# Depthwise convolution of a decoder trunk: shifted copies read from a DRAM copy of U, three buffers deep

## The chip, the cores and the metric

The kernel runs on one core of a Trainium2 chip. The metric is the device time of one execution in microseconds. Three runs of the kernel before took 2775.14, 2775.54 and 2778.75 us, median 2775.54 us.

## The reference

One inference step of a four-layer trunk for a prompt of 512 positions and for 8 decode streams of 4 positions each: 544 columns of 1024 channels. Layers 0 and 3 have a Conformer convolution as mixer, layer 1 latent attention, layer 2 retention; each layer then has a SwiGLU block. The change lies in the convolution, which is this:

```python
a = h @ w_pw1 + b_pw1
u = a[..., :D_MODEL] * jax.nn.sigmoid(a[..., D_MODEL:])
buf = jnp.concatenate([buf_prev.astype(u.dtype), u], axis=1)
c = lax.conv_general_dilated(buf, w_dw[:, None, :], (1,), 'VALID', ..., feature_group_count=D_MODEL) + b_dw
c = jax.nn.silu(_layernorm(c, ln_g, ln_b))
return c @ w_pw2 + b_pw2, buf[:, -(CONV_WIDTH - 1):]
```

Each of the 1024 channels has 31 taps of its own (CONV_WIDTH is 31); everything is in float32.

## The kernel before

Channels lie on the partitions, in eight tiles m = 0 to 7 of 128; columns lie along the free dimension. A column range is cut into two halves, h = 0 and h = 1, of 272 columns. A full-precision product is made of three passes over operands that ScalarE and VectorE have split into a high and a low part (`wsplit`, lines 196 and 197).

`conv` runs in four stages.

1. The first pointwise product (line 216, tiles `pg` and `pa`) makes U, one tile m after another: 835 columns per channel, which hold the padded prompt and the eight decode windows with their 30 past rows (lines 826 and 828 write it). Meanwhile VectorE computes the taps of tiles 0 and 1 by multiply-add (line 846).
2. The taps of the other tiles go through TensorE. `windows(m, h)` makes S, a tile of 128 partitions by 4 groups of 32 channels: for each group g one DMA on SyncE's queue reads 32 partitions of U four times, each time one column further, so that partition 4c+s holds channel c shifted by s (line 860). A matmul with a 128x32 matrix of taps (W, line 868) then sums four taps at a time, and eight matmuls for each of four groups make 31 taps (line 896). For h = 1 S has 560 columns, since it holds the decode windows too (four copies of 280 KB), for h = 0 it has 300 (four of 150 KB), and for tiles 0 and 1 only the decode windows are copied (four of 144 KB, line 882 alone). The pool gives S of h = 0 and S of h = 1 two buffers each: a copy into one of them starts when the matmuls that read it last are done.
3. Each result leaves its PSUM bank by VectorE (line 909), is squared on ScalarE (line 915) and goes into two running sums (lines 913 and 916). `moments(h)` turns these into mean and variance (ones-matmuls of lines 924 and 925, then lines 926 to 930 and `rsqrt`, lines 261 to 265); `normed` normalises a tile, applies silu and splits it (lines 937 to 943). Four PSUM banks go round among all of these.
4. The second pointwise product: four tiles with h = 0 alone first (lines 1548 to 1550, tile `pw2h`), moments and normalisation of h = 1 beside them, then the rest (tile `pw`).

TensorE's order around the convolutions is: decode window of tile 0, (2,0), (3,0), decode window of tile 1, (4,0), (5,0), (6,0), (2,1), (3,1), moments of h = 0, (4,1), (5,1), (6,1), (7,1), `pw2h` of tile 0, moments of h = 1; a pair is (m, h). Half (7,0) is made by VectorE, whose 31 multiply-adds are strewn between its other work (line 846). A framework sets each engine's order and its semaphores from the order of the code; each engine then runs its list strictly in order. SyncE's list also has the weight loads (line 188, two `raw` buffers).

Of the kernel before, what the change touches and what calls it, by code (L numbers as in the profile page):

```python
# [15 lines left out]
F = mybir.dt.float32  # L16
# [7 lines left out]
P = 128  # L24
D = 1024
KD = D // P
# [17 lines left out]
UW = SW + 3  # L44
# [92 lines left out]
class Trunk:  # L137
# [306 lines left out]
    def ffn(self, l, last, order):  # L444
# [14 lines left out]
        with ExitStack() as es:  # L459
# [97 lines left out]
            def four(w, f, put):  # L557
# [12 lines left out]
                def whole(out, op, x, y):  # L570
                    def sums():
                        a[out] = self.xsp.tile([P, 1024], F, tag="xs", name="S").rearrange("p (k c) -> p k c", k=4)
                        op(a[out], a[x], a[y])
# [183 lines left out]
    def conv(self, l, j):  # L757
        tc, nc, A, O = self.tc, self.nc, self.A, self.O
# [1 line left out]
        w2 = A["conv_w_pw2"][j].rearrange("(k p) c -> p k c", p=P)  # L760
        halves = (slice(0, HF), slice(HF, T))
        xs, R = self.enter(lambda k: self.col("norm_mix", l * KD + k))
        with tc.tile_pool(name=f"cv{j}", bufs=1) as cp:

            U = cp.tile([P, KD, UW], F, name="U")
            us = U[:, :, U0:SW].rearrange("p m (b q) -> p m b q", b=NB)
# [41 lines left out]
            for mp in range(0, KD, 2):  # L808
                rg = self.wload(w1[:, :, D + mp * P:D + (mp + 2) * P], KD, 256)
                ra = self.wload(w1[:, :, mp * P:(mp + 2) * P], KD, 256)  # L810
                for q in range(2):
                    m = mp + q
# [40 lines left out]
            def windows(m, h):  # L853

                c0, c1 = ((0, HF + 28), (HF, SW))[h]
                S = cp.tile([P, 4, c1 - c0], F, tag="S" + "AB"[h], name="S", bufs=2)
                a0 = U0 if h and m in CONV_DVE else c0
                for g in range(4):
                    src = U[g * 32:(g + 1) * 32, m, a0:c1]
                    nc.sync.dma_start(S[:, g, a0 - c0:], bass.AP(src.tensor, src.offset, [list(src.ap[0]), [1, 4], [1, c1 - a0]]))  # L860
                return S

            Ws = {}

            def diagonals(m):
                if m not in Ws:
                    W = self.wsp.tile([P, 1024], FR, tag="ws", name="W")[:, :].bitcast(F).rearrange("p (a b) -> p a b", a=32)
                    nc.vector.tensor_mul(W, diag.unsqueeze(1).to_broadcast([P, 32, 32]),
                                         tapst[:, m].rearrange("p g j -> p (g j)").unsqueeze(2).to_broadcast([P, 32, 32]))
                    Ws[m] = W  # L870
                return Ws[m]
# [5 lines left out]

            def sample(m, W, S, out):
                for i in range(8):
                    for g in range(4):  # L880
                        ss = S[:, g, U0 - HF:].rearrange("p (b q) -> p b q", q=SU)[:, :, 4 * i:4 * i + NT]
                        nc.tensor.matmul(out[g * 32:(g + 1) * 32, :], lhsT=W[:, g * 8 + i, :], rhs=ss, start=(i == 0), stop=(i == 7))

            def convolved(m, h):
# [6 lines left out]
                if on_pe:  # L891
                    W, S = diagonals(m), windows(m, h)
                    b = self.bank("cv")
                    for i in range(8):
                        for g in range(4):
                            nc.tensor.matmul(b[g * 32:(g + 1) * 32, :n], lhsT=W[:, g * 8 + i, :],  # L896
                                             rhs=S[:, g, 4 * i:4 * i + n], start=(i == 0), stop=(i == 7))
                    if h:
                        sample(m, W, S, b[:, n:HF])
# [46 lines left out]
            for i, m in enumerate(CO):  # L946
                if m < 7:
                    by_taps(7, 0, HF, range(at, at + SPR[i]))
                    at += SPR[i]
                if m in CONV_DVE:  # L950
                    b = self.bank("cvs")
                    sample(m, diagonals(m), windows(m, 1), b[:, :NS])
                    nc.scalar.activation(cc[m][:, TP:], b[:, :NS], AF.Identity, bias=bias(m))
                convolved(m, 0)
                if m == 0:
                    convolved(m, 1)
# [54 lines left out]
            for h in range(2):  # L1011
                b, s = self.bank("cpo"), self.bank("cso")
                for q in range(4):
                    m = h * 4 + q
# [886 lines left out]
```

## Time and profile before

| | before |
|---|---|
| median of three runs | 2775.54 us |
| profiled execution, its own time | 2779.04 us |
| its span in the trace | 2777.3 us |
| PE (TensorE) busy | 2725.3 us, 98% |
| DVE (VectorE) busy | 1912.0 us, 69% |
| ACT (ScalarE) busy | 1171.0 us, 42% |
| POOL (GpSimd) busy | 129.3 us, 5% |
| DMA of S from U, of the chain that ended last | 1% |
| SyncE's issue of line 860, of that chain | 1% |

A share of the span is a mean over stages with different limits. TensorE is busy for 98% of the whole, mostly with SwiGLU. The two convolution stages take a small part of the span, from about 128 to 206 us and from about 2264 to 2344 us, and what bounds them must be read there.

### The profile page before, as it was taken

What the parts mean: (1) busy time and instruction counts of PE and PEld (TensorE: products, weight loads), DVE (VectorE), ACT (ScalarE), POOL (GpSimd) and SP (SyncE); (2) the same over time, 40 slices, a digit from 0 to 9 for tenths busy, and PEclk for the clock granted to TensorE, in tenths of its full rate; (3) what the DMA queues carried; (4) which work ended last, traced back from release to release, by engine and by line L of the source; (5) the groups of instructions that cost most, each with busy time, mean ns of one, the idle gap of its engine ahead of it and who ended that gap; (6) DMA issues with size and microseconds to landing.
All of it is one profiled execution on the core that took longest, in us unless ns stands there. A gap on an engine that the chain in (4) does not pass through costs nothing.

```text
span 2777.3 us, 52103 instructions
## 1 busy us (share of the span) xinstructions
PE 2725.3 (98%) x22390; PEld 2550.4 (92%) x22390; DVE 1912.0 (69%) x2782; ACT 1171.0 (42%) x1713; POOL 129.3 (5%) x217
## 2 busy tenths in 40 slices
PE   8989999999999999999999999999999999999998
PEld 7969999998779999998888897999999977999998
DVE  6976667676775666677656565766667796756676
ACT  4145343454554343444434343534434315524445
POOL 1000000003420000000100000000000000000000
PEclk9999999999999999999999999999999999999999
DMA  5354332224333233223534334423232444423222
GB/s 158 108 136 138 100 98 92 92 76 140 95 113 107 91 94 105 92 74 104 171 116 158 131 131 136 151 79 107 92 100 68 116 122 129 138 77 107 93 84 86
DMA packets 220892, 305.64 MB, mean 110 GB/s; under 512 B 14911, under 2 KB 153484, under 8 KB 220630
## 3 DMA queue, kind: packets, MB, share of 16 engines
q1 hardware_dynamic: 209036, 266.84, 31.3%
q0 software_dynamic: 11328, 33.59, 3.6%
q8 instruction: 176, 2.88, 0.4%
q10 hardware_dynamic: 298, 1.88, 0.2%
q14 instruction: 54, 0.44, 0.0%
HBM read 256.51 MB, written 24.01 MB: 101 GB/s over the span
## 4 chain that ended last, share of the span: by engine, by line
PE 93%; DMA 3%; DVE 2%; SPq 1%; ACT 1%; issue 0%; ACTq 0%; DVEq 0%
PE p L216 28%; PE x L553 24%; PE pg L216 7%; PE pqk L216 3%; PE pa L216 3%; PE pwo L216 3%; PE pw L216 2%; PE po L216 2%; PE cv L896 2%; DMA S<-U 1%; PE pd L216 1%; PE pv L1548 1%; PE pv L1549 1%; PE pv L1550 1%; PE ob L1783 1%; SPq L860 1%
## 5 line engine op out<-in xcount | busy, mean ns | idle before, releaser
L484 ACT CAST wh<-raw 128x1024 fp32r<-128x1024 f32 (+1 forms) x236 | 241.3, 1022 | 411.9 <-PE p L216 267.7
L472 DVE TENSOR_TENSOR wl<-raw,wh 128x1024 fp32r<-128x1024 f32 (+1 forms) x236 | 279.5, 1184 | 76.1 <-ACT wh L484 75.6
L196 ACT CAST wh<-raw 128x1024 fp32r<-128x1024 f32 (+2 forms) x170 | 160.7, 949 | 378.7 <-PE pg L216 83.5
L216 PE MATMUL p<-gh,wl 128*128 128x272 f32 x1344 | 297.8, 288 | 0.0
L216 PE MATMUL p<-gh,wh 128*128 128x272 f32 x1344 | 297.1, 288 | 0.0
L553 PE MATMUL x<-Bh,wh 128*128 128x272 f32 x1792 | 296.9, 287 | 0.0
L553 PE MATMUL x<-Bh,wl 128*128 128x272 f32 x1792 | 296.8, 287 | 0.0
L216 PE MATMUL p<-gl,wh 128*128 128x272 f32 x1344 | 296.8, 288 | 0.0
L553 PE MATMUL x<-Bl,wh 128*128 128x272 f32 x1792 | 296.8, 287 | 0.0
L216 PE MATMUL p<-xs,wh 128*128 128x272 f32 x1536 | 256.9, 289 | 4.1 <-DVE t L295 4.1
L484 ACT CAST wh<-S 128x1024 fp32r<-128x1024 f32 x128 | 134.9, 1054 | 279.5 <-PE p L216 147.1
L553 PEld LDWEIGHTS x<-Bh,wh 128*128 128x128 f32 x1792 | 251.7, 188 | 0.0
L553 PEld LDWEIGHTS x<-Bh,wl 128*128 128x128 f32 x1792 | 251.5, 188 | 0.0
L553 PEld LDWEIGHTS x<-Bl,wh 128*128 128x128 f32 x1792 | 251.5, 188 | 0.0
L197 DVE TENSOR_TENSOR wl<-raw,wh 128x1024 fp32r<-128x1024 f32 (+2 forms) x170 | 185.4, 1094 | 73.8 <-ACT wh L196 54.7
L299 DVE TENSOR_TENSOR x<-p,x 128x544 f32<-128x544 f32 x152 | 110.0, 724 | 179.9 <-PE p L216 179.5
L216 PEld LDWEIGHTS p<-xs,wh 128*128 128x128 f32 x1536 | 217.5, 188 | 5.1 <-issue 2.8
L216 PEld LDWEIGHTS p<-gh,wh 128*128 128x128 f32 x1344 | 218.7, 188 | 0.0
L216 PEld LDWEIGHTS p<-gl,wh 128*128 128x128 f32 x1344 | 218.6, 188 | 0.0
L216 PEld LDWEIGHTS p<-gh,wl 128*128 128x128 f32 x1344 | 217.7, 189 | 0.0
L472 DVE TENSOR_TENSOR wl<-S,wh 128x1024 fp32r<-128x1024 f32 x128 | 156.6, 1223 | 70.9 <-ACT wh L484 70.9
L216 PE MATMUL pg<-xs,wh 128*128 128x272 f32 x1024 | 179.5, 293 | 5.2 <-ACT wh L196 5.2
(539 smaller groups left out, 5394.9 us busy)
## 6 DMA issues: line engine op xcount, KB each, us to landing
raw<-in_ffn_w SPq DMA_DIRECT2D x86, 1024.0 KB, 5.1
raw<-in_ffn_w SPq DMA_DIRECT2D x72, 512.0 KB, 3.9
raw<-in_conv_w_pw SPq DMA_DIRECT2D x28, 1024.0 KB, 5.6
state<-in_state_ret SPq DMA_DIRECT2D x32, 512.0 KB, 4.9
out_ret_state_sample<-state POOLq DMA_DIRECT2D x32, 512.0 KB, 3.6
S<-U SPq DMA_DIRECT2D x48, 280.0 KB, 5.4
raw<-in_ffn_w SPq DMA_DIRECT2D x16, 768.0 KB, 4.5
raw<-in_ret_w_v SPq DMA_DIRECT2D x8, 1024.0 KB, 5.0
```

What stands on the lines that cost most here:

```text
L196: self.nc.scalar.copy(hv, raw)
L197: self.nc.vector.tensor_sub(lv, raw, hv.bitcast(F))
L216: nc.tensor.matmul(ps[:M, h, :HF], lhsT=w[:, k, :], rhs=x[:, h * HF:(h + 1) * HF], start=(j == 0 and i == 0), stop=(j == n - 1 and i == 2))
L299: self.nc.vector.tensor_add(x, ps[:, :, :HF], x)
L472: nc.vector.tensor_sub(out, a, flat(h))
L484: nc.scalar.copy(job.w[0], src())
L553: nc.tensor.matmul(out[:, t, :HF], lhsT=a[:, k, m], rhs=b[:, k, :], start=(first and i == 0 and k == 0), stop=(i == 2 and k == 3), skip_gr ...
L860: nc.sync.dma_start(S[:, g, a0 - c0:], bass.AP(src.tensor, src.offset, [list(src.ap[0]), [1, 4], [1, c1 - a0]]))
L896: nc.tensor.matmul(b[g * 32:(g + 1) * 32, :n], lhsT=W[:, g * 8 + i, :], rhs=S[:, g, 4 * i:4 * i + n], start=(i == 0), stop=(i == 7))
L1548: nc.tensor.matmul(out, lhsT=ah, rhs=bh, start=start, stop=False)
L1549: nc.tensor.matmul(out, lhsT=ah, rhs=bl, start=False, stop=False)
L1550: nc.tensor.matmul(out, lhsT=al, rhs=bh, start=False, stop=stop)
```

## The change

`conv` gets a pool in DRAM with eight buffers. The first time that `windows` is called for a tile m, GpSimd's queue copies the whole tile of U (128 partitions by 835 columns, 428 KB) into one of them; the four copies of S, still on SyncE's queue, read the same elements from there. S has three buffers for each half instead of two. Lines after 863 move by three.

```diff
-        with tc.tile_pool(name=f"cv{j}", bufs=1) as cp:
+        with tc.tile_pool(name=f"cv{j}", bufs=1) as cp, tc.tile_pool(name=f"ud{j}", bufs=KD, space=bass.MemoryType.DRAM) as dp:
...
-                S = cp.tile([P, 4, c1 - c0], F, tag="S" + "AB"[h], name="S", bufs=2)
+                S = cp.tile([P, 4, c1 - c0], F, tag="S" + "AB"[h], name="S", bufs=3)
                 a0 = U0 if h and m in CONV_DVE else c0
+                if m not in Ud:
+                    Ud[m] = dp.tile([P, UW], F, tag="ud", name="ud")
+                    nc.gpsimd.dma_start(Ud[m], U[:, m, :])
                 for g in range(4):
-                    src = U[g * 32:(g + 1) * 32, m, a0:c1]
+                    src = Ud[m][g * 32:(g + 1) * 32, a0:c1]
                     nc.sync.dma_start(S[:, g, a0 - c0:], bass.AP(src.tensor, src.offset, [list(src.ap[0]), [1, 4], [1, c1 - a0]]))
                 return S
 
-            Ws = {}
+            Ws, Ud = {}, {}
```

SyncE's list in layer 0, before, from the copies for (2,0) to the weights of the second product; 300 columns are h = 0, 560 are h = 1:

```order
L860 DMA S<-U 128x1x300 x4
L188 DMA raw<-in_conv_w_pw 128x8x256
L860 DMA S<-U 128x1x300 x4
L188 DMA raw<-in_conv_w_pw 128x8x256 x3
L860 DMA S<-U 128x1x560 x4
L860 DMA S<-U 128x1x300 x8
L860 DMA S<-U 128x1x560 x4
L860 DMA S<-U 128x1x300 x4
L860 DMA S<-U 128x1x560 x16
L188 DMA raw<-in_conv_w_pw 128x8x256 x4
```

The same stretch of SyncE's list after the change; 288 columns are the decode windows of tile 1:

```order
L863 DMA S<-ud 128x1x300 x4
L188 DMA raw<-in_conv_w_pw 128x8x256
L863 DMA S<-ud 128x1x300 x4
L188 DMA raw<-in_conv_w_pw 128x8x256
L863 DMA S<-ud 128x1x288 x4
L863 DMA S<-ud 128x1x560 x4
L863 DMA S<-ud 128x1x300 x4
L188 DMA raw<-in_conv_w_pw 128x8x256 x2
L863 DMA S<-ud 128x1x560 x4
L863 DMA S<-ud 128x1x300 x8
L863 DMA S<-ud 128x1x560 x16
```

The copies for (2,1) and (4,0), which stood behind the first two loads of the second product's weights, now stand ahead of them; behind them follow (3,1), then (5,0) and (6,0), then (4,1) to (7,1). The decode windows of tile 1 stood earlier in the list and now stand behind (3,0). In layer 3 the list is the same.

GpSimd's list at the same place, before:

```order
L769 MEMSET U 128x8x3
L771 MEMSET U 128x8x2 x8
L779 MEMSET taps 128x8
L1020 DMA out_conv_state_prompt<-pr 30x1024
L1022 DMA out_conv_state_sample<-sr 4x1024 x8
```

and after:

```order
L771 MEMSET U 128x8x2 x8
L779 MEMSET taps 128x8
L860 DMA ud<-U 128x835 x8
L1023 DMA out_conv_state_prompt<-pr 30x1024
L1025 DMA out_conv_state_sample<-sr 4x1024 x8
```

The eight copies of U, in the order of tiles 0, 2, 3, 1, 4, 5, 6, 7, stand where GpSimd had nothing between the clearing of U's margins and the output of the convolution's state. VectorE's and ScalarE's lists keep their order; TensorE's keeps it but for one matmul of `pw2h`, which stood three matmuls into (7,1) and now stands behind it.

## Rows read from the trace of the kernel before

**Rows 1.** The page, part 1: busy time, share of the span, instructions.

```profile
PE 2725.3 (98%) x22390; PEld 2550.4 (92%) x22390; DVE 1912.0 (69%) x2782; ACT 1171.0 (42%) x1713; POOL 129.3 (5%) x217
```

**Rows 2.** Waits of SyncE's queue: who waited for whom, total us, times, longest.

```profile
SPq L860 <- PE cvs L882: 33.4, 4, 16.2
SPq L860 <- PE cv L882: 31.6, 5, 13.2
```

**Rows 3.** Timeline of VectorE, layer 0: start, us, instruction, idle before and its releaser.

```profile
151.12 2.10 DVE L846 SCALAR_TENSOR_TENSOR cc<-U,taps,cc 128x272 f32<-128x272 f32 x4
157.78 0.50 DVE L909 SCALAR_TENSOR_TENSOR cc<-cv,vec,K 128x272 f32<-128x272 f32 x1 [4.55 <-PE cv L896]
...
165.40 0.50 DVE L909 SCALAR_TENSOR_TENSOR cc<-cv,vec,K 128x272 f32<-128x272 f32 x1 [1.76 <-PE cv L882]
...
173.72 0.50 DVE L909 SCALAR_TENSOR_TENSOR cc<-cv,vec,K 128x272 f32<-128x272 f32 x1 [1.90 <-PE cv L882]
...
179.96 0.50 DVE L909 SCALAR_TENSOR_TENSOR cc<-cv,vec,K 128x272 f32<-128x272 f32 x1 [1.88 <-PE cv L882]
...
186.12 0.50 DVE L909 SCALAR_TENSOR_TENSOR cc<-cv,vec,K 128x272 f32<-128x272 f32 x1 [1.01 <-PE cv L882]
...
192.70 0.50 DVE L909 SCALAR_TENSOR_TENSOR cc<-cv,vec,K 128x272 f32<-128x272 f32 x1 [3.45 <-PE cv L882]
```

**Rows 4.** The same timeline in layer 3.

```profile
2281.59 0.50 DVE L909 SCALAR_TENSOR_TENSOR cc<-cv,vec,K 128x272 f32<-128x272 f32 x1 [1.60 <-PE cv L896]
...
2294.55 0.50 DVE L909 SCALAR_TENSOR_TENSOR cc<-cv,vec,K 128x272 f32<-128x272 f32 x1 [4.41 <-PE cv L896]
...
2302.17 0.50 DVE L909 SCALAR_TENSOR_TENSOR cc<-cv,vec,K 128x272 f32<-128x272 f32 x1 [1.76 <-PE cv L882]
...
2312.17 0.50 DVE L909 SCALAR_TENSOR_TENSOR cc<-cv,vec,K 128x272 f32<-128x272 f32 x1 [3.58 <-PE cv L882]
...
2316.77 0.50 DVE L909 SCALAR_TENSOR_TENSOR cc<-cv,vec,K 128x272 f32<-128x272 f32 x1 [0.24 <-PE cv L882]
...
2325.70 0.50 DVE L909 SCALAR_TENSOR_TENSOR cc<-cv,vec,K 128x272 f32<-128x272 f32 x1 [3.77 <-PE cv L882]
...
2330.87 0.50 DVE L909 SCALAR_TENSOR_TENSOR cc<-cv,vec,K 128x272 f32<-128x272 f32 x1 [2.04 <-PE cv L882]
```

**Rows 5.** Timeline of TensorE, layer 0; one convolution window is 64 records of line 896.

```profile
130.47 7.54 PE L896 MATMUL cv<-S,W 128*32 128x272 f32 x128
137.82 0.77 PE L882 MATMUL cvs<-S,W 128*32 128x32 f32 x64
...
161.36 3.45 PE L896 MATMUL cv<-S,W 128*32 128x240 f32 x64
...
165.29 0.72 PE L924 MATMUL s<-S,ones 128*128 128x272 f32 x2
...
195.59 0.62 PE L924 MATMUL s<-S,ones 128*128 128x272 f32 x2
```

**Rows 6.** DMA from 160 to 184 us, copies of S alone: rate, queue's engine share.

```profile
DMA packets 1941, 3.93 MB, mean 164 GB/s; under 512 B 208, under 2 KB 208, under 8 KB 1938
...
q1 hardware_dynamic: 1938, 3.88, 77.4%
```

**Rows 7.** The same from 64 to 70 us, a weight load from DRAM.

```profile
DMA packets 1979, 2.03 MB, mean 338 GB/s; under 512 B 69, under 2 KB 1977, under 8 KB 1977
```

**Rows 8.** Instructions on tile S: time from a copy's issue to its landing.

```profile
DMA to landing us min/median/max: 2.8/4.9/7.7
```

**Rows 9.** The page, part 6: GpSimd's stores of retention state, KB each, us to landing.

```profile
out_ret_state_sample<-state POOLq DMA_DIRECT2D x32, 512.0 KB, 3.6
```

**Rows 10.** Timeline of SyncE's queue in the first product of layer 0.

```profile
83.68 2.52 SPq L860 DMA_DIRECT2D S<-U  x4
88.92 24.33 SPq L188 DMA_DIRECT2D raw<-in_conv_w_pw  x3
```

**Rows 11.** The chain that ended last, there.

```profile
110.65 6.03 PE pa L216 x48
```

## The prediction

> **What bounds the kernel now.** The page comes first, and it misleads: TensorE is busy 98% of the span [rows 1], so an edit to copies seems worth nothing. The waits of SyncE's queue say where to look: the copies of S (line 860) waited 33.4 + 31.6 = 65.0 us for matmuls of the convolution, nine times [rows 2]. With two buffers, a copy starts only when the window two places earlier has been consumed, and TensorE then waits for that copy: a ring.
>
> The next view is VectorE's timeline in the convolution stages, since every window leaves PSUM through VectorE's line 909 and every later step hangs on the sums. Up to 153.22 us (151.12 + 2.10) VectorE works without a row of idle time from the stage's start. From there it sits idle six times in layer 0, each time ended by TensorE's last matmul of a window: 4.55 + 1.76 + 1.90 + 1.88 + 1.01 + 3.45 = 14.55 us [rows 3]. In layer 3 it is seven times: 1.60 + 4.41 + 1.76 + 3.58 + 0.24 + 3.77 + 2.04 = 17.40 us [rows 4]. So VectorE waits for TensorE, and TensorE waits for copies.
>
> TensorE's timeline shows what windows cost when S is there. Two windows with h = 0 take from 130.47 to 137.82 us, 3.68 each; one with h = 1, its decode part included, from 161.36 to 165.29, 3.93 us; a decode window alone 0.77 [rows 5].
>
> **The change, step by step.** The third buffer lets a copy start one window earlier. I follow layer 0 with the orders as they are built, on the axis of the old trace.
>
> TensorE, if S is there: the decode part of tile 1 ends at 137.82 + 0.77 = 138.6; (4,0), (5,0), (6,0) end at 138.6 + 3 x 3.68 = 149.6; (2,1) and (3,1) at 157.5. The moments of h = 0 then wait for the sum over all tiles, which VectorE finishes 4.4 us after 153.22 (an estimate: line 909 of (6,0), the last multiply-adds and two sums, ten instructions of about 0.4), so about 157.7; with some 1.2 us for four ones-matmuls, (4,1) starts at 158.9, and (4,1) to (7,1) end at 162.8, 166.7, 170.7 and 174.6.
>
> VectorE, if its idle times go: the next line 909 comes as early as the work before it allows. The work between two waits is the distance of their rows less the wait: 165.40 - 1.76 - 157.78 = 5.86, then 6.42, 4.36, 5.15 and 3.13 us [rows 3]. So line 909 runs at 153.22 for (6,0), 159.1 for (3,1), 165.5 for (4,1), 169.9 for (5,1), 175.0 for (6,1) and 178.1 for (7,1). TensorE is ahead each time, by 3.6, 1.6, 2.7, 3.2, 4.3 and 3.5 us. So all 14.55 us of idle time go, VectorE is the bound of the stage, and what is late next is VectorE's own work.
>
> The copies, if they land in time. From the end of the window that frees a buffer to the start of the one that needs it there are: (5,0), freed by (2,0) at 134.1, needed at 142.3, 8.2 us; (6,0) 8.1; (4,1) 20; (5,1), freed by (2,1) at 153.5, needed at 162.8, 9.3; (6,1) 9.2; (7,1), freed by (4,1) at 162.8, needed at 170.7, 7.9. No row shows a copy of S from DRAM, so I bound it. From below, the present copies: 164 GB/s at 77.4% of the engines' time, or 212 GB/s with the engines always busy [rows 6]; four copies of 280 KB, 1.147 MB, take 5.4 us, and with the shortest landing of a single copy, 2.8 us [rows 8], 8.2 us. From above, a weight load from DRAM: 338 GB/s [rows 7], so 3.4 + 2.8 = 6.2 us. I take 338, since the source is the same memory, and keep 212. At 338 every slack holds. At 212 the three last copies queue on the engines: (6,1) lands at about 167.1 and (7,1) at 172.5, 0.4 and 1.8 us after TensorE wants them, but VectorE asks for those windows at 175.0 and 178.1, 3.93 us after the latest start that does no harm (171.1 and 174.2). So either pace gives the same time: the third buffer is what pays, the source is not.
>
> [...]
>
> The added copies of U: eight of 428 KB per layer, on GpSimd's queue. The nearest row is a store of 512 KB from that queue, 3.6 us from issue to landing [rows 9]; from below it cannot gain anything, since a copy of S now waits for it. Seven of the eight lie in the first product, with TensorE's matmuls as cover. Queued behind them on SyncE are weight loads: the copies for (3,0) were issued at 83.68, when U's tile was done, and the next load at 88.92 [rows 10]. Now the copy of U goes at 83.68, S at 87.3, and with its four issues of 2.52 us the load at 89.8, 0.9 us later; TensorE's product of that load runs at 110.65 [rows 11], so it costs nothing. A store would have to take some 15 us before TensorE felt it. Tile 7's copy of U goes when the first product has ended, about 25 us before S is built from it. I cost these at nothing. GpSimd and TensorE have no other new wait; the second product's weights stay ahead of their use.
>
> Layer 3 has the same orders, so its 17.40 us go as well. Sum: 14.55 + 17.40 = 31.95 us. Made against the profiled execution (2779.04 us, 1.7 above its span) that gives 2747.1 us; the median of the runs is 3.5 us below that execution, so the forecast is 2775.54 - 31.95 = 2743.6 us.
>
> **The rivals.**
>
> - Hand-overs take the place of the waits. VectorE and ScalarE pass a window back and forth (909, 915, 916; then 937 to 943), and once VectorE has no slack each pass can show. For it: after 153.22 us no multiply-adds are left to fill in. Against it: the six stretches of work above hold these passes already, and are unbroken or nearly so. If each of the 13 waits leaves 0.8 us, 10.4 us come back: 2754 us. This needs no slow copy.
> - Nothing moves. The wait is only renamed: S waits for the copy of U instead of for a buffer, or SyncE's strict order puts a late load ahead of S. For it: SyncE's list now holds a wait for a store ahead of weight loads. Against it: the slacks of 15 and 25 us. It would give 2770 to 2781.
> - It gets slower, by one mechanism: the engines read S from DRAM slowly, because each row is read four times, each time 4 bytes further, right after it was written, and no row shows that. From 130.47 us on, five windows of 1.147 MB and two of 0.614 MB, 6.96 MB, must land before (7,1). That window left PSUM at 192.70 [rows 3], so its matmuls began 3.93 us earlier, at about 188.7; less 2.8 us for a landing that leaves 55.4 us. So below 126 GB/s the new kernel is slower than the old; the gain begins to shrink below 192 (three windows, 3.44 MB, between 153.5 and 174.2 less 2.8). At 100 GB/s the stage takes 14.2 us more per layer: 2804 us. Against it: 338 GB/s on rows half as long [rows 7].
> - More is gained: with earlier sums the normalisation, the second product or the loads of SwiGLU move up by more than the idle times. VectorE's own work forbids more than a few us: 2736 to 2740.
>
> **How the numbers follow.** Forecast, 2740 to 2748: 62%. Hand-overs, 2748 to 2760: 22%. More: 7%. Nothing, within 0.2%: 4%. Slower: 5%. A measurement of this kernel can tell 0.2%, 5.6 us, from no change. The range 2738 to 2756 takes in the forecast, most of the first rival's side and a part of the last one's, about 8 in 10; the tails left out are a pace below 192 GB/s and a gain above 37 us. Faster by over 0.2%: 62 + 22 + 7 = 91, and 1 from the edge of the third case, 92%; within 0.2% 3%; slower 5%.
>
> **What would show it.** In the profile after: VectorE's rows of line 909 for (6,0), (3,1) and (4,1) to (7,1) follow the row before them without idle time, and the stage from the first window to the ones-matmuls of h = 1, 65.1 us in layer 0 (130.47 to 195.59 [rows 5]), is 50.6 long, the same in layer 3. TensorE's waits for DMA of S are gone or below 2 us in all, and where TensorE waits in the stage, VectorE or ScalarE releases it. The copies of S run at over 212 GB/s of busy engine time; if not, the reason of the source is wrong and the time still holds. SyncE's queue still waits for matmuls, but one window further back. Copies of U land within 6 us of issue. The prediction is wrong if line 909 still waits for TensorE by more than 5 us per layer, if a weight load of the first product comes late, or if TensorE's wait for S stays above 10 us.

## The result and the profile after

| | before | after |
|---|---|---|
| median | 2775.34 us (2774.98 to 2778.75, 4 runs) | 2745.64 us (2743.08 to 2748.85, 4 runs) |
| profiled execution, span | 2779.04, 2777.3 us | 2744.18, 2742.4 us |
| first window to moments of h = 1, layer 0 | 65.1 us | 49.4 us |
| the same, layer 3 | 68.1 us | 49.4 us |

The two stages after are read to some 0.1 us: the first ones-matmul of h = 1 starts at 180.13 and at 2298.40 us, 0.1 us before the windows shown below end.

The ratio is 0.9889, with a 95% interval of 0.9877 to 0.9901: 29.7 us less between medians, 34.9 between the two profiled executions. The prediction, 2743.6 us (2738 to 2756), holds. Lines after 863 stand three higher now: VectorE's 909 is 912, TensorE's 896 is 899, SyncE's 860 is 863.

The page's first part, which answers to [rows 1], is again the view that tells least; TensorE is still the busy engine.

```profile
PE 2704.0 (99%) x22390; PEld 2547.3 (93%) x22390; DVE 1910.9 (70%) x2782; ACT 1170.3 (43%) x1713; POOL 137.5 (5%) x233
```

VectorE's timeline in layer 0 answers to [rows 3]. Columns: start, duration, instruction, and in brackets any idle time ahead of it.

```profile
153.53 0.50 DVE L912 SCALAR_TENSOR_TENSOR cc<-cv,vec,K 128x272 f32<-128x272 f32 x1
157.89 0.50 DVE L912 SCALAR_TENSOR_TENSOR cc<-cv,vec,K 128x272 f32<-128x272 f32 x1
159.30 0.49 DVE L912 SCALAR_TENSOR_TENSOR cc<-cv,vec,K 128x272 f32<-128x272 f32 x1
165.62 0.49 DVE L912 SCALAR_TENSOR_TENSOR cc<-cv,vec,K 128x272 f32<-128x272 f32 x1
169.91 0.49 DVE L912 SCALAR_TENSOR_TENSOR cc<-cv,vec,K 128x272 f32<-128x272 f32 x1
...
174.97 0.49 DVE L912 SCALAR_TENSOR_TENSOR cc<-cv,vec,K 128x272 f32<-128x272 f32 x1
...
177.65 0.44 DVE L946 TENSOR_TENSOR cs<-cc,cs 128x272 fp32r<-128x272 f32 x1 [0.78 <-ACT cs L945]
178.01 0.49 DVE L912 SCALAR_TENSOR_TENSOR cc<-cv,vec,K 128x272 f32<-128x272 f32 x1
```

No bracket is left at the line that had six. One hand-over to ScalarE shows, 0.78 us, ahead of line 946. It is not new: before, VectorE waited the same 0.78 us for ScalarE ahead of line 943, in both layers.

The windows view gives both stages: length, busy time of each engine (with its instructions), granted clock, DMA share, GB/s.

```profile
core 0: us, PE busy (x) PEld busy (x) DVE busy (x) ACT busy (x) POOL busy (x), PEclk, DMA share, GB/s
130.85:180.25 49.40, 47.10 (x1182) 34.47 (x1182) 48.21 (x116) 21.79 (x44) 0.54 (x1) 1.00 0.56 174
2249.10:2298.50 49.40, 47.93 (x1182) 34.96 (x1182) 48.21 (x116) 21.67 (x44) 0.54 (x1) 1.00 0.55 174
```

VectorE is busy for 48.21 of 49.40 us: the bound. TensorE is 1.1 us of work behind it, or 0.3 in layer 3. The same view of before:

```profile
130.47:195.59 65.12, 56.20 (x1182) 34.38 (x1181) 48.83 (x116) 20.83 (x43) 0.00 (x0) 0.97 0.66 153
2265.70:2333.80 68.10, 58.50 (x1182) 37.12 (x1182) 48.92 (x116) 20.74 (x43) 0.00 (x0) 0.92 0.62 146
```

VectorE's work is the same, 48.8 and 48.2; what went is the rest.

The granted clock (the column PEclk, as a share of full speed) shows a part of that rest which is no wait for a copy. In four stretches of the stages before it was 0.50: from about 152 to 155.5 us in layer 0, and in layer 3 three times for about as long, from 2289, 2306 and 2319.5 us. Two of them, from the kernel before:

```profile
152.00:155.00 3.00, 3.00 (x26) 1.19 (x28) 1.16 (x3) 0.00 (x0) 0.00 (x0) 0.52 0.00 0
2320.00:2323.00 3.00, 3.00 (x30) 1.76 (x32) 1.93 (x4) 1.16 (x3) 0.00 (x0) 0.50 0.98 240
```

Ahead of these four TensorE had just stood idle, for 2.9 us in layer 0 and for 1.4 and 1.1, 2.0 and 2.0 us in layer 3, and each lies in a window whose end one of VectorE's long waits was for: 4.55 [rows 3], 4.41, 3.58 and 3.77 us [rows 4]. In the first of them TensorE was at half its pace: 30 matmuls in the 3.43 us from 152.04, against 65 in the 3.63 us from 130.47 at a clock of 1.00. At that pace a stretch of some 3.4 us loses about 1.7 us, by an estimate from these figures, some 7 of the 31.9 us in all. After the change no such stretch is left in either stage.

The chain that ended last shows it once more. A piece of before, in order of time (start, duration, what):

```profile
164.36 1.85 SPq L860
...
168.55 1.15 SPq L860
169.74 6.17 DMA S<-U
175.96 3.06 PE cv L896 x57
...
179.39 0.55 PE cv L882 x35
179.99 0.54 SPq L860
...
181.23 6.58 DMA S<-U
187.85 0.59 PE cv L896 x2
```

Matmuls free a buffer, SyncE issues, the copy lands, matmuls run: one turn of the ring. After, the chain from 131 to 180 us goes along VectorE and holds neither a copy nor line 899:

```profile
131.81 0.75 DVE U L826
133.40 0.41 DVE cc L846
...
149.64 0.41 DVE cc L912
151.58 0.42 DVE cc L846
...
158.94 0.44 DVE S L919
```

TensorE's waits after (engine, line, waited for: us, times, longest) have no DMA of S among them:

```profile
PE s L927 <- DVE S L916: 2.5, 2, 1.5
...
PE cv L899 <- issue: 1.2, 1, 1.2
```

SyncE's queue still waits, now for the copy of U as well. It waits earlier, and TensorE shows no wait for it; these rows answer to [rows 2]. The waits for matmuls, 65.0 us before, are still 57.6: their total was no measure of what they cost.

```profile
SPq L863 <- DMA ud<-U: 43.6, 8, 10.0
SPq L863 <- PE cvs L885: 31.6, 2, 16.2
SPq L863 <- PE cv L885: 26.0, 6, 9.5
```

The copies of S themselves, from 153 to 168 us:

```profile
DMA packets 1707, 3.44 MB, mean 229 GB/s; under 512 B 185, under 2 KB 185, under 8 KB 1705
...
q1 hardware_dynamic: 1705, 3.41, 71.8%
```

3.41 MB in 15 us at 71.8% of the engines' time is 317 GB/s when busy, against 212 before [rows 6] (209 if only the 3.88 MB of S are counted, as here; the prediction took the bytes of all queues).

### The profile page after: what moved, and what is told of

Read it like the earlier page. It is cut to its first block, busy times and chain, and to the rows that moved or that the text cites. A ratio compares the mean times of both kernels' runs of the same rounds, so it can differ in the third digit from the quotient of the medians.

```text
span 2742.4 us, 52128 instructions
## 1 busy us (share of the span) xinstructions
PE 2704.0 (99%) x22390; PEld 2547.3 (93%) x22390; DVE 1910.9 (70%) x2782; ACT 1170.3 (43%) x1713; POOL 137.5 (5%) x233
## 4 chain that ended last, share of the span: by engine, by line
PE 91%; DVE 5%; DMA 2%; ACT 1%; issue 1%; SPq 0%; ACTq 0%; DVEq 0%
PE p L216 28%; PE x L553 25%; PE pg L216 7%; PE pqk L216 4%; PE pa L216 3%; PE pwo L216 3%; PE po L216 2%; PE pw L216 2%; PE pd L216 1%; PE pv L1551 1%; PE pv L1552 1%; PE pv L1553 1%; PE ob L1786 1%; DMA raw<-in_ffn_w 1%; DVE cc L846 1%; DMA raw<-in_conv_w_pw 1%
```

## The experiments

My theory: the ring of two buffers cost the time, the third buffer gives it back, and the source of the copies does not matter. The rival: the faster copies pay. A second question is what bounds the stage now.

**The third buffer alone.** Two buffers become three in the kernel before; U stays in SBUF.

```diff
-                S = ... name="S", bufs=2)
+                S = ... name="S", bufs=3)
```

> The kernel before with three buffers of S instead of two; the copies still come from U in SBUF. Theory 1 (the third buffer is what pays): VectorE runs through the multiply-adds without idle time, the stage from the first window to the ones-matmuls of the moments takes 49 to 51 us in both layers as in the kernel after (49.4), the time is 2745 us (2741 to 2750), and the copies still move about 212 GB/s of the time that their queue is busy. Theory 2 (the pace of the copies pays, the kernel after has 319 GB/s): the copies stay late, VectorE still waits over 5 us in each layer, and the time is 2760 us or more.

Measured: 2744.43 us (2743.12 to 2746.01), ratio to before 0.9884 [0.9869, 0.9900], as the kernel after. The line of VectorE over the whole trace (count, busy, mean ns, idle before), in the kernel before and here, the page's row of the copies, and the DMA view from 157 to 172 us:

```profile
L909 DVE SCALAR_TENSOR_TENSOR cc<-cv,vec,K 128x272 f32<-128x272 f32 x22 | 10.9, 498 | 31.9 <-PE cv L882 21.4 <-PE cv L896 10.6
L909 DVE SCALAR_TENSOR_TENSOR cc<-cv,vec,K 128x272 f32<-128x272 f32 x22 | 10.9, 494 | 0.0
```
```profile
S<-U SPq DMA_DIRECT2D x48, 280.0 KB, 5.4
```
```profile
q1 hardware_dynamic: 1531, 3.04, 86.6%
```

The idle time went from 31.9 to 0.0 us while a copy of 280 KB lands after 5.4 us as before; 3.04 MB in 15 us at 86.6% is 234 GB/s. TensorE waits 1.8 us for S in all. Theory 1 holds, and the trip through DRAM is not needed.

**The source alone.** The kernel after with two buffers.

```diff
-                S = ... name="S", bufs=3)
+                S = ... name="S", bufs=2)
```

> The kernel after with two buffers of S: only the source of the copies is changed, each tile of U goes to DRAM once and S is read from there. Theory 1: the ring of two still makes each copy wait for the matmuls of the pair two before it, but the copy itself lands faster, so a part of VectorE's 31.95 us of idle time goes: 2760 us (2754 to 2768), with 5 to 10 us of idle time left in each layer. Theory 2 (the pace is what counts): 2744 to 2750 us, idle time under 2 us in each layer. A third: the two passes through DRAM take as long together as the slower copy, and it stays at 2775 us.

Measured: 2759.55 us (2756.09 to 2763.45), ratio 0.9935 [0.9921, 0.9949]: 16.5 us, half of the gain.

```profile
L912 DVE SCALAR_TENSOR_TENSOR cc<-cv,vec,K 128x272 f32<-128x272 f32 x22 | 11.0, 499 | 16.7 <-PE cv L885 12.1 <-PE cv L899 4.6
```

16.7 us of idle time are left, 5.3 in layer 0 and 11.4 in layer 3, where 5 to 10 in each were expected. With two buffers a faster copy shortens each turn of the ring, and the pace does count; with three, at 234 and at 317 GB/s, it does not. The two parts of the change overlap and do not add: 31.6 and 16.5 alone, 29.7 together.

**Why the old copies were slow.** Before, with every fourth partition as the source of each copy (channels in another order).

```diff
-                    src = U[g * 32:(g + 1) * 32, m, a0:c1]
+                    src = U[g::4, m, a0:c1]
```

> The kernel before, two buffers, source in SBUF, but each of the four copies takes every fourth of the 128 partitions instead of 32 neighbouring ones (so the channels come in another order than the reference's). If it is the 32 neighbouring partitions that hold the copies at 212 GB/s: 300 GB/s or more of busy time and the time of the kernel with the DRAM source and two buffers, about 2760 us. If it is the SBUF source as such, or the writing into S: 212 GB/s and 2775 us as before.

Measured: 2757.70 us (2754.41 to 2760.87), ratio 0.9933 [0.9919, 0.9946], the time of the DRAM source. From 157 to 172 us:

```profile
q1 hardware_dynamic: 1714, 3.41, 61.7%
```

3.41 MB in 15 us at 61.7% is 368 GB/s when busy, against 200 in the same stretch before (1.69 MB at 56.4%) and 212 [rows 6], out of the same memory and into the same S. So the 32 neighbouring partitions held the copies back, not SBUF as a source. Why the neighbours give less, no row shows.

**What bounds the stage now.** The kernel after with taps 10 to 21 of half (7,0) left out, and the kernel before with the same taps left out; VectorE has about 5 us less work per layer.

```diff
                 for k in ks:
+                    if m == 7 and 10 <= k < 22:
+                        continue
```

> The kernel after with taps 10 to 21 of the multiply-adds of one half (m = 7, h = 0) left out: 12 instructions of VectorE, about 4.9 us in each layer. Theory 1 (VectorE bounds the stage, 48.2 of its 49.4 us busy; TensorE is busy for 47.1 and 47.9 and is next): the stage falls to 47 to 48.5 us, the time by 2 to 5 us to 2742 us (2740 to 2744). Rival (TensorE or the copies bound the stage already): the stage stays at 49.4 us and the time at 2745.5 us, and VectorE shows about 4.9 us more of idle time in each layer.

> The kernel before (two buffers) with taps 10 to 21 of the multiply-adds of one half (m = 7, h = 0) left out: the same 12 instructions of VectorE, 4.9 us per layer, that were left out of the kernel after. Theory 1 (with two buffers the copies and the matmuls that wait for them bound the stage, VectorE only waits at its end): 2775 us as before (2772 to 2777), and VectorE's idle time ahead of line 911 (line 909 before) grows from 31.95 to about 38 to 42 us. Rival (VectorE's own work bounds the stage in the kernel before as well): 2766 us.

Measured: after 2742.32 us (2739.54 to 2743.93), ratio to before 0.9875 [0.9860, 0.9890]; before 2775.19 us (2770.84 to 2779.94), ratio 0.9996 [0.9987, 1.0005]. The stage of the first, and VectorE's line of the second:

```profile
131.42:179.05 47.63, 46.90 (x1181) 34.51 (x1181) 43.14 (x104) 21.07 (x44) 0.54 (x1) 1.00 0.57 180
```
```profile
L911 DVE SCALAR_TENSOR_TENSOR cc<-cv,vec,K 128x272 f32<-128x272 f32 x22 | 11.0, 501 | 36.8 <-PE cv L884 23.8 <-PE cv L898 12.9
```

After the change the stage shrinks by 1.7 us in layer 0 (49.28 to the first ones-matmul, now 47.63) and by 1.4 in layer 3, until TensorE's 46.9 us are the bound; 3.3 us of the time follow, in medians whose intervals overlap, so the stage is the stronger evidence. Before the change the same cut buys nothing in the medians (0.6 us), and idle time grows, from 31.9 to 36.8 us. 38 to 42 were expected: half of the 10 us left out does not show at this line. The stages of this profiled execution are 63.1 and 65.4 us long, 2.0 and 2.7 less than in the one of before, but it lies 3.4 us below its median and that of before 3.7 above, so these two traces do not settle the other half. VectorE became the bound by the change.

**Relieving VectorE by GpSimd.** Three buffers, U in SBUF, the last three of the eight matrices W built by GpSimd.

```diff
-                    nc.vector.tensor_mul(W, ...
+                    (nc.vector if len(Ws) < 5 else nc.gpsimd).tensor_mul(W, ...
```

> Three buffers of S from U in SBUF, and the last three of the eight diagonal matrices W (line 868) built by GpSimd instead of VectorE; two of these builds, 1.2 us each, stand in the stage. Theory 1 (VectorE bounds the stage by 48.2 of 49.4 us, TensorE is next at 47): the stage falls to 47.3 to 48 us, the time to 2741 us (2738 to 2744). Rival (GpSimd builds W late or slows VectorE beside it): TensorE waits for W or VectorE's 0.41 us per multiply-add grows, 2746 to 2756 us.

Measured: 2748.01 us (2745.56 to 2751.29), ratio to before 0.9894 [0.9879, 0.9909]: no gain, 3.6 us above three buffers alone. GpSimd's timeline, then VectorE's:

```profile
128.62 5.02 POOL L868 TENSOR_TENSOR W<-diag,tapst 128x1024 f32<-128x1024 f32 x2 [109.41 <-PE pa L216]
138.48 2.02 POOL L868 TENSOR_TENSOR W<-diag,tapst 128x1024 f32<-128x1024 f32 x1 [4.84 <-PE cvs L882]
```
```profile
130.28 1.58 DVE L826 SCALAR_TENSOR_TENSOR U<-ta,vec,tg 128x512 f32<-128x512 f32 x1
131.79 1.90 DVE L828 SCALAR_TENSOR_TENSOR U<-ta,vec,tg 128x32 f32<-128x32 f32 x1
...
138.64 2.15 DVE L846 SCALAR_TENSOR_TENSOR cc<-U,taps,cc 128x272 f32<-128x272 f32 x1
```

Beside GpSimd's builds three instructions of VectorE stretch, line 828 to 1.90 us; two of them end as GpSimd's spans do (133.69 against 133.64, 140.79 against 140.50). With three buffers alone line 828 took 0.25 us and line 846 a mean of 0.49. VectorE's stage is 1.3 us busier (49.5 against 48.2) with three builds less. The rival's second half was right.

**How far the pace matters.** Three buffers, and beside each copy of S a second one of the same bytes from the same place into a scratch in DRAM, on GpSimd's queue: once from U in SBUF, once from the copy of U in DRAM.

```diff
                     nc.sync.dma_start(S[:, g, a0 - c0:], ...)
+                    nc.gpsimd.dma_start(again.tile([P, c1 - a0], ...), ...)
```

> Three buffers, source U in SBUF, and beside each copy into S a second copy of the same bytes from the same 32 partitions to a scratch in DRAM that nothing reads, on GpSimd's queue. The two share what the source gives, 212 GB/s, so S gets about 106 GB/s. The 28 copies of the stage (20 of 287 KB, 8 of 154 KB, 7.0 MB) need 66 us at that pace. Theory 1 (the pace costs nothing until the copies fill the stage): now it does, TensorE waits for S over 10 us in each layer, and the time is 2765 to 2790 us. Rival (the pace never matters with three buffers): 2745 us, the waits for S below 2 us.

> The kernel after, and beside each copy into S a second copy of the same bytes from the same place in DRAM to another scratch in DRAM that nothing reads, on GpSimd's queue. If the two share 319 GB/s evenly, S gets 160 GB/s, and the 7.0 MB of the stage need 44 us of its 49. Theory 1: just within the stage, some waits for S of 1 to 3 us in each layer, 2746 to 2754 us. Rival (any loss of pace shows): 2760 us or more.

Measured: 2786.50 us from SBUF (2780.11 to 2788.73), ratio 1.0032 [1.0017, 1.0047], a time as expected, with 10.1 us of TensorE's waits for S in layer 0 and 9.3 in layer 3, where over 10 in each were expected; 2767.84 us from DRAM (2766.26 to 2769.80), ratio 0.9966 [0.9952, 0.9979], 14 us above my range, with waits of 5.0 and 6.6 us where I expected 1 to 3. The queues of the second kernel from 142 to 153 us (q0 the added copies, q1 those of S: packets, MB, share of the engines), and its page's row of the copies of h = 0:

```profile
q0 software_dynamic: 845, 3.03, 74.9%
q1 hardware_dynamic: 868, 0.95, 27.3%
```
```profile
S<-ud SPq DMA_DIRECT2D x40, 150.0 KB, 6.5
```

In these 11 us the engines were full and did not share the bytes evenly: the added copies moved 275 GB/s, S 86, not the 160 I had counted on. What was even is the number of packets, 845 and 868; a packet of the added copies held 3.6 KB, one of S 1.1. From SBUF, in the same stretch, it was 602 and 540 packets, 196 and 79 GB/s. A copy of 150 KB landed after 6.5 us, 8.0 from SBUF, where 2.9 and 3.7 were usual, and one copy of S from DRAM took 16.8 us (144.09 to 160.92).

Both kernels lose against three buffers alone. But the edit did not halve the pace throughout: the added copies wait for no buffer of S, so they ran ahead; the last were issued by 166 us, and from 168 to 180 us S had the engines all but to itself (4.4 us a copy). On the same queue they also held up the copy of U for tile 7, issued at 152.29 us instead of 133.35. So these runs set no one pace for the stage and do not test the 126 GB/s below which the prediction saw the new kernel slower than the old: the one from DRAM is still 8 us faster than before. I had also compared the total, 44 us of copies in 49; but the ring asks each window to land within some 8 us. Which of these errors weighs more, these runs don't separate.

**Each half's third buffer alone.** Before, with three buffers for the second half only, then for the first half only.

```diff
-                S = ... name="S", bufs=2)
+                S = ... name="S", bufs=(2, 3)[h])
```

> The kernel before with three buffers of S for the windows of the second half of the columns (h = 1, 280 KB a copy) and still two for those of the first half. In the trace before, VectorE's waits that fall into the second half are 1.76, 1.90, 1.88, 1.01 and 3.45 us in layer 0 and 1.76, 3.58, 0.24, 3.77 and 2.04 us in layer 3, 21.4 us together; those of the first half are 4.55 and 1.60 and 4.41 us, 10.6 us together. Theory 1 (each half waits for its own ring): the 21.4 us go and the 10.6 us stay, 2754 us (2751 to 2757). Rival (SyncE issues all copies in one order, so that a copy of the first half that waits for its buffer holds up those of the second half behind it): part of the second half's waits stays, 2758 to 2770 us.

> The kernel before with three buffers of S for the windows of the first half (h = 0, 150 KB a copy) and still two for the second half. Theory 1 (each half waits for its own ring): the first half's 10.6 us of waits go, the second half's 21.4 us stay, 2765 us (2762 to 2768). Rival (one order of copies): the second half's copies hold up all, and little goes, 2769 to 2775 us.

These two ran on a chip on which the kernel before took 2801.17 us, so only ratios count: 0.9948 [0.9935, 0.9962] for the second half, 2786.26 us, which is 14.4 us on the scale of 2775.5; 0.9951 [0.9938, 0.9965] for the first, 2787.30 us, 13.6 us. 21 and 11 were expected of theory 1. The lines of VectorE, second half's buffer first:

```profile
L909 DVE SCALAR_TENSOR_TENSOR cc<-cv,vec,K 128x272 f32<-128x272 f32 x22 | 10.9, 495 | 13.2 <-PE cv L896 9.2 <-PE cv L882 4.0
```
```profile
L909 DVE SCALAR_TENSOR_TENSOR cc<-cv,vec,K 128x272 f32<-128x272 f32 x22 | 10.9, 497 | 16.2 <-PE cv L882 16.2
```

13.2 us are left against 10.6 expected, 16.2 against 21.4. With the second half's buffer the first half's wait stays (4.03 in layer 0) and so does the wait right behind it, 1.68 where it was 1.76 [rows 3]. With the first half's, the waits of the second half that come soon after it shrink (1.76 to 0.33 in layer 0), the late ones stay. So the halves are coupled and theory 1 sized both wrong. That SyncE's one order does the coupling is a reading, not shown; the rival with its 2758 to 2770 us is nearer for the second half, theory 1 for the first. Both buffers are needed.

A third buffer also acts ahead of the stage, which the theories left out. SyncE's queue, before and after (start, duration, what), from the end of the first product on:

```profile
129.50 54.85 SPq L860 DMA_DIRECT2D S<-U  x36
```
```profile
129.84 35.52 SPq L863 DMA_DIRECT2D S<-ud  x28
```

36 copies of S were still to be issued in the stage before, 28 are after and with both third buffers alone, and 32 with either one of them: each lets four more copies go during the first product. How much of the gain is this head start, and how much the deeper ring in the stage, no run separates; nor does one hold the order of SyncE's list, which changes with the buffers, apart from them.

## Why the prediction was right

- The ring and what breaks it. Right: the third buffer alone gives 31.6 us, the DRAM source alone 16.5, and the chain turns from copies to VectorE.
- All of VectorE's idle time goes. Right at the line it named: 31.9 us to 0.0. Line 912 was forecast at 153.2, 159.1, 165.5, 169.9, 175.0 and 178.1 us; it came at 153.53, 159.30, 165.62, 169.91, 174.97 and 178.01, on an axis on which the stage starts 0.4 us later (130.85 for 130.47).
- The stage becomes 50.6 us in both layers. It became 49.4. VectorE's whole idle time in layer 0 was 65.12 - 48.83 = 16.3 us, not the 14.55 of line 909 alone: some 1.7 lay ahead of other lines. 49.40 - 48.21 = 1.2 us of it stayed, and VectorE's own work took 0.6 us less. Layer 3 gained 18.7 us in this way, not 17.4.
- The sum. The stages gave 15.7 + 18.7 = 34.4 of the 34.9 us between the profiled executions; the start moved by 0.4 us, the stretch between the stages by -1.3 and the end by 0.4. The medians differ by 29.7, since the profiled execution of before lay 3.7 us above its median and that of after 1.5 below. The forecast made against medians, 31.95, is 2.2 us high. That it came so near is in part luck: the stages gave 2.5 us more than the sum had, and the sum took the idle times of an execution slower than the median and set them against the median, an error of the other sign.
- The clock. The prediction gave the idle times to the copies alone. TensorE's four stretches at a granted clock of 0.50, some 7 us by the estimate above, were in them too; since the waits ahead of these stretches went, they went with them, and the sum is not touched. That such a stretch follows an idle time, and goes with it, the rows show for this stage; why only some idle times have one, they do not.
- The source does not matter. Right with three buffers; at 234 and at 317 GB/s the times are 2744.43 and 2745.64 us. The rates are 200 to 234 from 32 neighbouring partitions of SBUF, 317 from DRAM, and 368 from SBUF once the partitions are spread. DRAM was the faster source only against the neighbouring partitions.
- The copies of U cost nothing. Right in time, wrong in one size: they landed after 4.7 us at the median and 6.0 at most (3.6 forecast), and the weight load behind them went out at 93.12 us instead of 88.92 [rows 10], 4.2 us later (0.4 of them the later start), not 0.9. TensorE has no wait for it.

```profile
90.55 2.47 SPq L863 DMA_DIRECT2D S<-ud  x4
93.12 0.54 SPq L188 DMA_DIRECT2D raw<-in_conv_w_pw  x1
```

- The rivals. None was needed, at 2745.64 us. Hand-overs show with 0.78 us in each stage, not 0.8 at each wait, and that wait stood there before. The slow-copy rival has its place: slowed by second copies from SBUF the kernel is slower than before, by 11 us. Its price, 28 us at 100 GB/s, is not tested, since the copies had no one pace.

## What to carry to other kernels

Where an engine waits for transfers that themselves wait for that engine, count the buffers before the bandwidth: one more buffer was worth all of the gain here, a copy half as fast again about half of it and, beside the buffer, nothing. Read the gain as the idle time of the engine that will be the bound next (VectorE's 31.9 us), and take all of its idle time in the stage, not only that of one line. The version to keep is the simplest, three buffers with U in SBUF: 2744.43 us against 2745.64, within the noise, without a copy of U or a pool in DRAM.

## What the runs showed of the hardware

- The pace of the copies of S went with the partitions they read from: 200 to 234 GB/s of busy time out of 32 neighbours (the kernel before, and with the third buffer alone), 368 out of every fourth of 128.
- Beside GpSimd's builds of W, VectorE's line 828 took 1.90 us, against 0.25 with three buffers alone; two of the three stretched instructions end within 0.05 and 0.29 us of GpSimd's spans. Why they stretch, no row shows.
- From 142 to 153 us of the run with second copies from DRAM, with the engines full (74.9% and 27.3%), the two queues moved nearly as many packets each and not as many bytes: 845 and 868 packets, 275 and 86 GB/s, at 3.6 and 1.1 KB a packet.
- The mean granted clock of layer 0's stage was 1.00 after the change, with the third buffer alone, with the DRAM source alone and with the spread partitions. Before it was 0.97, and 0.92 in layer 3, with four stretches of about 3.4 us at 0.50 in the two stages, each behind idle times of 1.1 to 2.9 us; others, such as 1.39 us ahead of 168.39, were followed by none. With the second copies from DRAM and from SBUF, where TensorE waited 5.0 and 10.1 us for S, it was 0.94 and 0.88 in layer 0.
